# A whole hybrid decoder trunk, its instructions ordered by a different model machine

## Chip, cores and metric

The kernel runs on one core of a Trainium2 chip. The metric is the device time of one execution in microseconds, the median of the runs.

## The reference

Two layers work on a sequence of 512 rows of 1024 channels, in float32. Each layer is a feed-forward half step, a mixing step and another feed-forward half step. Every step begins with an RMS norm that is scaled and shifted by values from a conditioning vector c (`mod = silu(c) @ w_ada + b_ada`), and ends with a gated residual.

```python
hn = rms_norm(h, g_ffn1[l]) * (1.0 + sc1) + sh1
h = h + 0.5 * (1.0 + gt1) * swiglu(hn, w_ffn1_in[l], w_ffn1_out[l])   # 1024 -> 2 x 2816 -> 1024
hn = rms_norm(h, g_mix[l]) * (1.0 + sc2) + sh2
proj = hn @ w_mix_in[l]
mixed = concatenate([attention, rwkv7, short_conv]) @ w_mix_out[l]
h = h + (1.0 + gt2) * mixed
# and a second swiglu with g_ffn2, w_ffn2_in, w_ffn2_out
```

Mixing splits its projection in three: sliding-window attention with sinks over 8 heads, an RWKV-7 recurrence over 4 heads, and a gated short convolution.

## The kernel before

All activations lie transposed, channels on partitions, in 8 tiles `h` of 128 x 512. A float32 weight is not multiplied as it is: ScalarE casts it to a rounded high part `wH` (L101), VectorE subtracts to get the low part `wL` (L102), and TensorE adds up the three products high-high, high-low and low-high (`mm3` from L87, `mm6` from L94). So each weight goes through a load into `wraw` (L267, two buffers), `first`, `third` or `sum` (L391), a cast, a subtraction, and then TensorE; `wH` and `wL` have four buffers each.

The stages follow each other as they are traced: `begin` (the first norm and the first four products, with a number of products of ones to keep TensorE going, `ps_warm`, L1197), then for each layer `ffn`, `mix`, `ffn`. In `ffn`, some row pairs of the inner width are made plainly by `projector`, and the rest by `pair_in`, which saves products by adding weights and activations beforehand; some of these weight sums are made by a DMA that accumulates, issued by GpSimd (L395). The conditioning values are dot products on VectorE (L163), 128 of them over weights that GpSimd's queue loads (`wada`, L177), laid between the other work. In `mix`, `products` yields the big weight products step by step, and three generators, `rwkv(0)`, `rwkv(1)` and `attention`, yield between small products and vector work. A loop with a running credit traces them in turn. The recurrence's part of interest: `ps_o` (L964 to L969), `RT` on VectorE (L971), the copy of `y` on ScalarE (L972), six steps `ps_s` and `St` (L977, L978), `ps_ys` (L983), then a group norm.

What runs when on an engine isn't the traced order. A list scheduler walks through a model machine's time: whenever an engine is free in the model, the ready instruction that was traced first is put next, and buffers of a pool are given out in the same walk. The order it finds is then fixed for each engine's queue, with semaphores for what depends on another engine. Only in some places is the order laid down by hand: regions `tc.manual_schedule` (for instance in `close`, for VectorE and ScalarE, and around some groups of small products) and `tc.issue_after`. The model machine thus decides the rest of the order.

## Time and profile before

| | us |
|---|---|
| median of 3 runs (lowest, highest) | 1912.97 (1912.38, 1913.72) |
| the profiled execution | 1913.21 |
| its span, first to last instruction | 1911.2 |
| TensorE busy | 1878.8 |
| VectorE busy | 1399.8 |
| ScalarE busy | 837.0 |
| GpSimd busy | 130.7 |

Busy time is the union of an engine's instructions. TensorE's matmuls overlap in its pipeline, so a row's mean duration is longer than the distance between two of them. In a row of waits stand the waiting engine, tile and line, what ended the wait, the total in us, the count and the longest. In a row of the order in time stand the start in us, the duration, what ran, the count, and in brackets the idle time of the engine before it with what ended it.

### The profile page before, as it was taken

What the parts mean: (1) busy time and instruction counts of PE and PEld (TensorE: products, weight loads), DVE (VectorE), ACT (ScalarE), POOL (GpSimd) and SP (SyncE); (2) the same over time, 40 slices, a digit from 0 to 9 for tenths busy, and PEclk for the clock granted to TensorE, in tenths of its full rate; (3) what the DMA queues carried; (4) which work ended last, traced back from release to release, by engine and by line L of the source; (5) the groups of instructions that cost most, each with busy time, mean ns of one, the idle gap of its engine ahead of it and who ended that gap; (6) DMA issues with size and microseconds to landing.
All of it is one profiled execution on the core that took longest, in us unless ns stands there. A gap on an engine that the chain in (4) does not pass through costs nothing. (4 is left out here: it accounts for less than half of the span.)

```text
span 1911.2 us, 37042 instructions
## 1 busy us (share of the span) xinstructions
PE 1878.8 (98%) x15504; PEld 1741.7 (91%) x15504; DVE 1399.8 (73%) x2181; ACT 837.0 (44%) x1264; POOL 130.7 (7%) x212
## 2 busy tenths in 40 slices
PE   8999999999999999999999999999999999999999
PEld 7998899897888999899899989989878899988998
DVE  7687687758976877677877776876599667864862
ACT  4443255346322554155345514544562235532551
POOL 0101100100000001110100020010000000110000
PEclk8999999999999999999999999999999999999999
DMA  7767877521312476887727678781321315774741
GB/s 300 245 168 221 271 198 229 168 70 45 79 43 81 123 198 176 278 218 199 264 62 193 171 260 242 191 278 42 93 61 49 88 34 163 209 217 130 198 140 59
DMA packets 104326, 308.46 MB, mean 161 GB/s; under 512 B 23392, under 2 KB 24416, under 8 KB 103136
## 3 DMA queue, kind: packets, MB, share of 16 engines
q1 hardware_dynamic: 75936, 203.33, 32.9%
q0 software_dynamic: 28224, 102.77, 21.7%
q8 instruction: 121, 1.98, 0.4%
q14 instruction: 45, 0.37, 0.1%
HBM read 302.66 MB, written 3.41 MB: 160 GB/s over the span
## 5 line engine op out<-in xcount | busy, mean ns | idle before, releaser
L101 ACT CAST wH<-wraw 128x1024 fp32r<-128x1024 f32 (+2 forms) x292 | 268.4, 922 | 512.6 <-PE ps_mm L91 176.8
L102 DVE TENSOR_TENSOR wL<-wraw,wH 128x1024 fp32r<-128x1024 f32 (+2 forms) x292 | 308.1, 1058 | 96.9 <-ACT wH L101 95.8
L90 PE MATMUL ps_mm<-actH,wH 128*128 128x512 f32 (+1 forms) x784 | 288.5, 368 | 0.0
L91 PE MATMUL ps_mm<-actL,wH 128*128 128x512 f32 (+1 forms) x784 | 288.0, 367 | 0.0
L92 PE MATMUL ps_mm<-actH,wL 128*128 128x512 f32 (+1 forms) x784 | 288.0, 367 | 0.0
L441 PE MATMUL ps_d<-comH,wH 128*128 128x256 f32 x816 | 226.8, 278 | 1.6 <-ACT wH L101 0.8
L443 PE MATMUL ps_d<-comH,wL 128*128 128x256 f32 x816 | 225.8, 277 | 2.3 <-DVE wL L102 2.3
L442 PE MATMUL ps_d<-comL,wH 128*128 128x256 f32 x816 | 225.5, 276 | 0.0
L98 PE MATMUL ps_mm<-hnH,wH 128*128 128x256 f32 x1040 | 214.0, 286 | 5.1 <-ACT hnH L101 2.9
L98 PE MATMUL ps_mm<-hnL,wH 128*128 128x256 f32 x1040 | 211.8, 283 | 0.0
L98 PE MATMUL ps_mm<-hnH,wL 128*128 128x256 f32 x1040 | 209.5, 281 | 0.5 <-DVE wL L102 0.5
L163 DVE SCALAR_TENSOR_TENSOR wada<-wada,crep 128x1024 f32<-128x1024 f32 x140 | 168.0, 1220 | 47.8 <-DMA wada<-in_wadaT 47.6
L102 DVE TENSOR_TENSOR wL<-sum,wH 128x1024 fp32r<-128x1024 f32 x102 | 124.8, 1224 | 74.9 <-ACT wH L101 74.7
L98 PEld LDWEIGHTS ps_mm<-hnH,wH 128*128 128x128 f32 x1040 | 159.5, 190 | 16.1 <-issue 8.2
L92 PEld LDWEIGHTS ps_mm<-actH,wL 128*128 128x128 f32 x784 | 147.8, 189 | 24.4
L90 PEld LDWEIGHTS ps_mm<-actH,wH 128*128 128x128 f32 x784 | 147.8, 189 | 24.2
L91 PEld LDWEIGHTS ps_mm<-actL,wH 128*128 128x128 f32 x784 | 147.8, 189 | 24.1
L101 ACT CAST wH<-sum 128x1024 fp32r<-128x1024 f32 x102 | 107.5, 1054 | 140.3 <-PE ps_d L442 60.1
L98 PEld LDWEIGHTS ps_mm<-hnL,wH 128*128 128x128 f32 x1040 | 160.2, 190 | 6.7 <-issue 5.7
L98 PEld LDWEIGHTS ps_mm<-hnH,wL 128*128 128x128 f32 x1040 | 160.1, 190 | 4.1 <-issue 2.9
L441 PEld LDWEIGHTS ps_d<-comH,wH 128*128 128x128 f32 x816 | 153.2, 188 | 3.9 <-ACT wH L101 1.4
L443 PEld LDWEIGHTS ps_d<-comH,wL 128*128 128x128 f32 x816 | 153.2, 188 | 2.9 <-DVE wL L102 2.9
(402 smaller groups left out, 4237.3 us busy)
## 6 DMA issues: line engine op xcount, KB each, us to landing
wada<-in_wadaT POOLq DMA_DIRECT2D x128, 512.0 KB, 4.9
wraw<-in_wmi SPq DMA_DIRECT2D x40, 512.0 KB
wraw<-in_w2p SPq DMA_DIRECT2D x36, 512.0 KB
wraw<-in_w1p SPq DMA_DIRECT2D x32, 512.0 KB
wraw<-in_w1o SPq DMA_DIRECT2D x32, 384.0 KB
wraw<-in_w2o SPq DMA_DIRECT2D x32, 384.0 KB
wraw<-in_w1i SPq DMA_DIRECT2D x20, 512.0 KB
wraw<-in_w1o SPq DMA_DIRECT2D x32, 320.0 KB
```

The lines of the kernel that those rows point to most:

```text
L90: mm(acc, wH, xH, start=start, stop=False)
L91: mm(acc, wH, xL, start=False, stop=False)
L92: mm(acc, wL, xH, start=False, stop=stop)
L98: mm(acc[:, sl], w[a][:, k], x[b][:, sl], start=start and n == 0 and sl is HALVES[0], stop=stop and n == 2, skip_group_check=True)
L101: nc.scalar.copy(hi, src)
L102: nc.vector.tensor_sub(lo, src, hi.bitcast(F32))
L163: stt(w, w, 1.0, crep, ALU.mult, ALU.mult, accum_out=out_)
L441: mm(pt[:, i], wH, x[k][0], start=start and i + k == 0, stop=False, skip_group_check=True)
L442: mm(pt[:, i], wH, x[k][1], start=False, stop=False, skip_group_check=True)
L443: last = mm(pt[:, i], wL, x[k][0], start=False, stop=k == 3, skip_group_check=True)
```

## The change

The kernel's first statement opens a block that holds the rest of the function, and asks that this block be ordered on the scheduler's other model machine. That one follows the queues, the sequencers and the transfers in time, where the default one has simpler times. The traced program is the same, with the same instructions, tiles, pools and hand-fixed regions. A block is scheduled as a unit; since all of the kernel lies in it, there is nothing outside for it to mix with.

```diff
 def trunk_kernel(ctx, tc, ins, out, layers=L, phases=("ffn1", "mix", "ffn2")):
     nc = tc.nc
+    ctx.enter_context(tc.block(schedule_with_timeline_sim=True))
     PSUM = bass.MemoryType.PSUM
     const = ctx.enter_context(tc.tile_pool(name="const", bufs=1))
     small_ = ctx.enter_context(tc.tile_pool(name="small", bufs=2))
```

## The prediction

> **What bounds the kernel now.** I read the page's first parts, then the busy time of stretches, then the waits of TensorE, and last the order in time around its longest stop.

> ```profile
> span 1911.2 us, 37042 instructions
> PE 1878.8 (98%) x15504; PEld 1741.7 (91%) x15504; DVE 1399.8 (73%) x2181; ACT 837.0 (44%) x1264; POOL 130.7 (7%) x212
> PE   8999999999999999999999999999999999999999
> PEclk8999999999999999999999999999999999999999
> ```

> TensorE is idle for 1911.2 - 1878.8 = 32.4 us of the whole program. That is all that a better order could hand back, beside time lost to a low clock. The profiled execution took 1913.21 us, 2.0 us more than its span and 0.24 us above the median of the three runs, 1912.97. The next view splits the idle time by stage; its columns are the stretch, its length, busy time with counts of each engine, granted clock, DMA share and GB/s.

> ```profile
> 0.00:22.40 22.40, 16.60 (x84) 14.03 (x84) 10.92 (x28) 12.35 (x20) 0.21 (x4) 0.98 0.89 343
> 22.40:37.00 14.60, 12.88 (x73) 12.38 (x74) 14.10 (x24) 6.85 (x10) 0.00 (x0) 0.68 1.02 415
> 399.00:622.00 223.00, 216.17 (x2433) 187.86 (x2434) 166.60 (x341) 92.97 (x193) 0.85 (x4) 1.00 0.24 67
> 1335.00:1558.00 223.00, 215.18 (x2415) 186.81 (x2416) 164.45 (x337) 92.30 (x192) 0.85 (x4) 0.99 0.24 67
> 700.00:750.00 50.00, 50.00 (x443) 50.00 (x443) 37.99 (x42) 27.72 (x36) 4.20 (x6) 1.00 0.67 180
> ```

> The two mixing stages (third and fourth row) hold 6.8 + 7.8 = 14.6 us of idle TensorE, the first 37 us hold 5.8 + 1.7 = 7.5 us, and a stretch in a feed-forward stage (last row) holds none. So the feed-forward stages run at what TensorE gives, and the order of instructions can only matter in the mixing stages and at the start, unless the new order takes away the cover that the feed-forward stages have. How thick is that cover? The waits of ScalarE and of TensorE tell it:

> ```profile
> ACT wH L101 <- PE ps_mm L91: 186.1, 70, 3.5
> ACT wH L101 <- PE ps_d L442: 85.8, 80, 3.7
> PE ps_d L443 <- DVE wL L102: 1.5, 2, 0.8
> PE ps_g L443 <- DVE wL L102: 1.1, 1, 1.1
> L101 ACT CAST wH<-wraw 128x1024 fp32r<-128x1024 f32 (+2 forms) x292 | 268.4, 922 | 512.6 <-PE ps_mm L91 176.8
> L102 DVE TENSOR_TENSOR wL<-wraw,wH 128x1024 fp32r<-128x1024 f32 (+2 forms) x292 | 308.1, 1058 | 96.9 <-ACT wH L101 95.8
> ```

> The weight splits wait for TensorE to give a buffer back (150 of them in the first two rows), not the other way round; TensorE waited for a split only a few times (rows three and four, at the heads of stages). wH and wL have four buffers each, so three weights stand ready when a fourth is freed.

> **The change part by part.** Nothing is added or removed on an engine; only the issue order on each engine can differ, with the buffers that follow from it. There are four places where that can cost.

> *Feed-forward stages.* A weight of a pair step is 24 matmuls of 256 columns; in the rows further below two such matmuls take 0.23 us, so a weight lasts 24 x 0.114 = 2.7 us and three ready ones 8.2 us. A split costs 0.92 + 1.06 = 2.0 us, which leaves some 6 us by which the new order may delay a split before TensorE notices. I take 0. Two rows give the ends: the last fortieth of the span, and the count of pair steps.

> ```profile
> 1863.40:1911.20 47.80, 44.02 (x251) 38.75 (x249) 12.39 (x18) 5.12 (x7) 0.00 (x0) 1.00 0.18 59
> L101 ACT CAST wH<-third x34: 1046/1052/1062, 126.6 to 1835.9; 128x1024 fp32r<-128x1024 f32 x34
> ```

> Of the 32.4 us idle, 14.6 lie in the mixing stages, 7.5 at the start and 47.8 - 44.0 = 3.8 at the end; the remaining 6.5 are the heads of the feed-forward stages, and no more can go there (-6.5). If each of the 34 pair steps paid a stop of the size seen at a stage head, 0.8, it would be +27.

> *Mixing stages.* Here chains of small products (two RWKV heads' groups, attention) are laid between weight products. TensorE's stops here, the first four of eleven rows of its waits between 399 and 622 us (layer 0), and the largest of layer 1:

> ```profile
> PE ps_s L977 <- ACT y L972: 1.4, 1, 1.4
> PE ps_bo L611 <- DVE bonus L800: 0.9, 2, 0.5
> PE ps_ks L611 <- ACT ksq L659: 0.8, 1, 0.8
> PE ps_pt L1057 <- DVE Sc L1050: 0.7, 2, 0.4
> PE ps_s L977 <- ACT y L972: 2.2, 1, 2.2
> ```

> Each such stop is a place where the order puts a chain step earlier than the chip can run it. The opposite error is hidden in these rows: a chain step that stands behind weight products although it is ready. It costs nothing at once, since TensorE works on, but it brings the end of the chain later, and once the weight products are used up that shows as idle time. One product step is six matmuls, three rows of the kind below:

> ```profile
> 1522.04 0.39 PE L98 MATMUL ps_mm<-y3H,wH 128*128 128x256 f32 x2
> 1522.27 0.39 PE L98 MATMUL ps_mm<-y3L,wH 128*128 128x256 f32 x2
> 1522.49 0.39 PE L98 MATMUL ps_mm<-y3H,wL 128*128 128x256 f32 x2
> 1522.72 0.39 PE L98 MATMUL ps_mm<-y4H,wH 128*128 128x256 f32 x2
> ```

> so 1522.72 - 1522.04 = 0.68 us. A chain of `rwkv` has 28 steps (its yields). If the other machine places q of them one product step later, the chain ends 0.68 q later. The two chains run side by side, so a layer pays once. Ends: q = 0, and q = 28, which is 19 us a layer or 38 in both. I take a quarter, q = 7, because the present order was early on the chip in the eleven kinds of places of that view, out of 76 chain steps (two times 28 and attention's 20), about one in seven, and a machine that errs to the other side as well will displace more than that: 7 x 0.68 = 4.8 us a layer, 9.5 us in both.

> *The longest stop.* It sits where the RWKV state recurrence starts, in both layers. VectorE, then ScalarE, then TensorE in layer 1:

> ```profile
> 1524.43 1.23 DVE L102 TENSOR_TENSOR wL<-wraw,wH 128x1024 fp32r<-128x1024 f32 x1 [4.26 <-ACT wH L101]
> 1525.58 0.75 DVE L971 TENSOR_TENSOR RT<-ps_o,AR 128x256 f32<-128x256 f32 x2
> 1523.35 1.05 ACT L101 CAST wH<-wraw 128x1024 fp32r<-128x1024 f32 x1 [5.22 <-DMA wraw<-in_wmo]
> 1526.03 0.70 ACT L972 COPY y<-ps_o 128x256 f32<-128x256 f32 x2 [1.62 <-DVE RT L971]
> 1526.45 0.33 PE L977 MATMUL ps_s<-St,GT 64*64 64x64 f32 x4 [2.17 <-ACT y L972]
> 1526.71 0.73 PE L98 MATMUL ps_mm<-y0H,wH 128*128 128x256 f32 x2
> 1527.24 0.63 PE L98 MATMUL ps_mm<-y0L,wH 128*128 128x256 f32 x2
> 1524.30:1526.40 2.10, 0.00 (x0) 0.00 (x0) 1.97 (x4) 0.48 (x3) 0.00 (x0) 1.00 0.00 0
> 1526.80:1530.20 3.40, 3.40 (x17) 3.06 (x18) 1.50 (x4) 0.66 (x1) 0.00 (x0) 0.50 0.55 146
> ```

> ScalarE's cast waits 5.2 us for a weight's DMA, VectorE's subtraction waits for the cast, and RT, which needs neither, is queued behind it; so the copy y and the first ps_s come late and TensorE stops for 2.17 us (1.4 in layer 0). After it the granted clock is 0.50 for 3.4 us, which is another 1.7 us. A machine that lets that DMA land later would put RT ahead of the subtraction: -(2.2 + 1.4 + 1.7) = -5.3 us. The same machine may as well put new waits of this form elsewhere, at the same price each. I count 0 here and keep -5.3 for a rival.

> [...]

> *The start.* The stretch 22.4 to 37 us ran at a mean granted clock of 0.68. A reordering can cost or save one such half-clock window, 3.4 / 2 = 1.7 us; I take +1.0 since warm-up products placed differently leave a longer stop more easily than a shorter one. Ends -2 and +5 (5.8 us are idle in the first 22.4).

> *The block's entry and exit.* The trace of before has none. Its nearest rows are the first wait of TensorE, for an operand made by an engine that has itself just begun, and the fetching of instructions:

> ```profile
> PE ps_warm L1197 <- ACT ones_r L130: 2.4, 1, 2.4
> q8 instruction: 121, 1.98, 0.4%
> ```

> The fetches go on all through the program beside other work. I take 0, with -1 and +3 as bounds (a second beginning of 2.4 us, rounded up).

> Sum: 1913.2 + 0 (feed-forward) + 9.5 (mixing) + 0 (longest stop) + 1.0 (start) + 0 (block) = 1923.7; less the 0.24 that this execution lies above the median, 1923.5, so 1924.

> **The rivals.** The measurement tells 0.2% (3.8 us) from no change: faster is below 1909.1, slower above 1916.8.

> *Faster.* The machine that follows the queues lets weights land late, so RT goes ahead of the subtraction in both layers (-5.3), and about half of the 6.5 us of feed-forward heads (-3) go with it: 1913.0 - 8 = 1905. For it: the stop is exactly of the form that a model without the DMA's wait would make, and it is there in both layers. Against it: it is only 8 of 32.4 us, and as few as 6 displaced chain steps in all (6 x 0.68 = 4.1 us) bring it back over 1909.1; that is the point from which it decides.

> *No change.* Both machines agree on what is ready where it matters, because in the feed-forward stages the buffers set the order and in the mixing stages the hand-fixed regions do: 1913. Against it: the mixing stages have many places free to move, and 15 us of stops show times that a second machine need not repeat.

> *Feed-forward stages disturbed.* SP and POOL issue in order. If a weight load that waits for a buffer is put ahead of one that could go, or an accumulating load on POOL behind a wada load that waits for VectorE, the cover of 6 us is used up. POOL's queue already stands still long:

> ```profile
> POOL wada L177 <- DVE wada L163: 278.6, 87, 22.4
> POOL third L395 <- DMA third<-in_w2p: 209.9, 16, 35.1
> ```

> With waits of up to 22 us there, one exchange passes through the cover. At one stop of 0.8 us in each of 34 pair steps it is +27 on top of 10.5: 1950; with clock windows lost, more.

> **How the numbers follow.** Mixing stages later (1917 to 1938): 0.40, time 1924. Faster by way of RT and the stage heads (1899 to 1909): 0.27. No change: 0.18. Feed-forward disturbed (1938 and up): 0.15. So faster 0.27, same 0.18, slower 0.55. The range: the faster rival's middle part from 1903, and up to 1955 for the disturbed case's nearer half; about 0.1 is left out at either end. The likeliest case's own range is 1917 to 1938.

> **What would show it.** Right: the stretch of 700 to 750 us still full; the mixing stages' stretches longer than before, with idle time in their last quarter, and ps_s (L977) first started later relative to the stage's begin. RT (L971) standing before the wL that precedes it now would be the faster rival. New rows of TensorE waiting for wL or wH in dozens would be the disturbed case. The sum fails if chain steps move ahead of product steps rather than behind, since then stops shrink or grow without a late chain end, or if the mixing stages' TensorE busy time itself changes because small products are grouped differently.

## The result, and the profile after

The changed kernel takes 1930.33 us (median of four runs, 1928.57 to 1932.86) beside 1913.35 for the kernel before: ratio 1.009, interval [1.0073, 1.0108], 17 us slower. The profiled execution is the fastest of the four, 1928.57 us with a span of 1926.5. Line numbers of the kernel are higher by one than before.

The head of the page and two of its rows by fortieths:

```profile
span 1926.5 us, 37060 instructions
PE 1874.1 (97%) x15504; PEld 1746.0 (91%) x15504; DVE 1392.1 (72%) x2181; ACT 844.1 (44%) x1268; POOL 130.8 (7%) x212
PE   8999999999998999999999999999999989999999
PEclk8999999999999999999999999999999989999999
```

TensorE is idle for 1926.5 - 1874.1 = 52.4 us instead of 32.4, and busy for 4.7 us less. The two eights in the inside of its row are the ends of the two mixing stages.

Stage by stage, from the first `ps_ks` of a mixing stage to the first pair product behind it, and on; before, then after (stretch, length, busy time of TensorE, its weight loads, VectorE, ScalarE and GpSimd, granted clock, DMA share, GB/s):

```profile
399.30:674.10 274.80, 268.27 (x2886) 239.96 (x2887) 210.20 (x413) 121.10 (x235) 2.59 (x6) 1.00 0.28 80
674.10:1335.70 661.60, 656.68 (x4794) 617.86 (x4792) 498.98 (x692) 299.07 (x403) 68.63 (x108) 1.00 0.68 199
1335.70:1612.20 276.50, 269.38 (x2886) 241.00 (x2887) 210.17 (x413) 121.18 (x235) 2.58 (x6) 0.99 0.28 79
1612.20:1911.20 299.00, 294.04 (x2102) 274.80 (x2100) 182.71 (x215) 121.52 (x156) 18.02 (x24) 1.00 0.57 157
```

```profile
399.90:681.70 281.80, 266.54 (x2887) 242.32 (x2888) 208.60 (x412) 123.02 (x236) 2.59 (x6) 0.98 0.26 76
681.70:1345.50 663.80, 656.71 (x4794) 617.75 (x4792) 496.73 (x694) 299.75 (x404) 68.70 (x108) 1.00 0.68 199
1345.50:1627.10 281.60, 266.62 (x2886) 242.36 (x2887) 208.88 (x413) 123.65 (x237) 2.60 (x6) 0.98 0.26 76
1627.10:1926.50 299.40, 293.57 (x2102) 274.53 (x2100) 181.37 (x216) 121.43 (x157) 18.03 (x24) 1.00 0.57 159
700.00:750.00 50.00, 50.00 (x443) 50.00 (x442) 40.26 (x44) 29.46 (x38) 5.07 (x7) 1.00 0.73 192
614.50:617.80 3.30, 3.30 (x17) 3.30 (x17) 0.69 (x1) 0.34 (x1) 0.00 (x0) 0.50 0.00 0
631.50:638.20 6.70, 4.81 (x22) 4.81 (x23) 6.19 (x14) 3.60 (x8) 0.00 (x0) 0.50 0.23 78
```

The mixing stages grew by 7.0 and 5.1 us, the feed-forward stretches by 2.2 and 0.4, everything ahead of the first mixing stage by 399.9 - 399.3 = 0.6: together the 15.3 us between the spans. In the mixing stages TensorE's idle time went from 274.8 - 268.3 = 6.5 to 15.3 us and from 7.1 to 15.0, while its busy time fell by 1.7 and 2.8, although (last two rows) 10 us of layer 0's stage now run at a granted clock of 0.50 (13.7 us of layer 1's, by the trace's record of the clock). The stretch of 700 to 750 us is full as before.

TensorE's largest waits in the changed kernel (waiting tile and line, what ended the wait, total, count, longest), and then the order in time on TensorE around the largest one in layer 0. Its first row is the first step of the first group's recurrence, the next three are steps of the second group's (the first, the second and the last):

```profile
PE ps_mm L99 <- DVE y L1002: 9.6, 2, 4.8
PE ps_mm L91 <- ACT hnH L251: 5.2, 3, 2.1
PE ps_av L1076 <- DVE pmp L1062: 4.3, 4, 1.6
PE ps_o L965 <- DVE N L955: 4.1, 2, 2.8
```

```profile
557.21 0.33 PE L978 MATMUL ps_s<-St,GT 64*64 64x64 f32 x4
...
586.95 0.33 PE L978 MATMUL ps_s<-St,GT 64*64 64x64 f32 x4
590.40 0.33 PE L978 MATMUL ps_s<-St,GT 64*64 64x64 f32 x4
...
602.52 0.33 PE L978 MATMUL ps_s<-St,GT 64*64 64x64 f32 x4
...
614.24 0.69 PE L99 MATMUL ps_mm<-yrH,wH 128*128 128x256 f32 x2 [4.78 <-DVE y L1002]
...
633.39 1.01 PE L91 MATMUL ps_mm<-hnH,wH 128*128 128x256 f32 x3 [2.10 <-ACT hnH L251]
```

The same rows of the two recurrences in the kernel before:

```profile
542.69 0.33 PE L977 MATMUL ps_s<-St,GT 64*64 64x64 f32 x4
...
589.11 0.33 PE L977 MATMUL ps_s<-St,GT 64*64 64x64 f32 x4 [1.36 <-ACT y L972]
591.45 0.33 PE L977 MATMUL ps_s<-St,GT 64*64 64x64 f32 x4 [0.44 <-DVE St L978]
...
598.21 0.33 PE L977 MATMUL ps_s<-St,GT 64*64 64x64 f32 x4
```

The second group's recurrence in layer 0 starts 2.2 us earlier, but from its first step to its last it takes 15.6 us instead of 9.1. By count of the trace, 26, 22, 22, 22 and 22 products of weights stand between the six steps, where before there were 12, 12, 9, 11 and 10. In layer 1 it takes 13.4 us instead of 10.1, with 22, 22, 24, 22 and 5 products between the steps. These products keep TensorE busy, so no wait shows there. But they are the products that were to cover the group norm behind the recurrence: now they are used up, and TensorE stops for 4.78 us until `y` is there, in each layer. A second stop is new in `close`, where the products of the norm (`ps_ss`, `ps_rstd`) stand behind the whole last weight sequence; the next stage's first operand `hnH` comes late by 2.10 us, in each layer.

A third place lies on VectorE ahead of the recurrence; its order in time in the changed kernel, where the first row is the subtraction for the second of the two last output weights:

```profile
574.51 1.23 DVE L103 TENSOR_TENSOR wL<-wraw,wH 128x1024 fp32r<-128x1024 f32 x1 [1.04 <-ACT wH L102]
576.51 3.35 DVE L993 RECIPROCAL gnrs<-gnrs 128x512 f32<-128x512 f32 x1 [0.78 <-ACT gnrs L992]
580.90 0.42 DVE L955 TENSOR_TENSOR N<-ps_gn,pc 128x256 f32<-128x256 f32 x1
585.41 0.75 DVE L972 TENSOR_TENSOR RT<-ps_o,AR 128x256 f32<-128x256 f32 x2
```

The first group's recurrence now starts 557.2 - 399.9 = 157.3 us into the stage, where it was 542.7 - 399.3 = 143.4. So its group norm now meets the second group's setup: its reciprocal takes 3.35 us ahead of `N`, for which `ps_o` waits 2.8 us (the wait list's last row). In the kernel before that reciprocal ran at 553.1 us, long before the second group's `N`.

### The profile page after: what moved, and what is told of

Read it like the earlier page. It is cut to its first block, busy times and chain, and to the rows that moved or that the text cites. A ratio compares the mean times of both kernels' runs of the same rounds, so it can differ in the third digit from the quotient of the medians.

```text
span 1926.5 us, 37060 instructions
## 1 busy us (share of the span) xinstructions
PE 1874.1 (97%) x15504; PEld 1746.0 (91%) x15504; DVE 1392.1 (72%) x2181; ACT 844.1 (44%) x1268; POOL 130.8 (7%) x212
## 3 DMA queue, kind: packets, MB, share of 16 engines
q1 hardware_dynamic: 75936, 203.33, 32.4%
q8 instruction: 121, 1.98, 0.4%
## 4 chain that ended last, share of the span: by engine, by line
PE 83%; DVE 9%; DMA 2%; issue 2%; ACT 2%; SPq 1%; POOL 0%; DVEq 0%; ACTq 0%; POOLq 0%
PE ps_mm L99 17%; PE ps_mm L92 9%; PE ps_mm L91 9%; PE ps_mm L93 9%; PE ps_d L444 6%; PE ps_d L442 6%; PE ps_d L443 6%; PE ps_f L442 3%; PE ps_f L444 3%; PE ps_f L443 3%; PE ps_g L444 2%; PE ps_g L443 2%; PE ps_g L442 2%; DVE wL L103 1%; SPq L860 1%
## 5 line engine op out<-in xcount | busy, mean ns | idle before, releaser
L102 ACT CAST wH<-wraw 128x1024 fp32r<-128x1024 f32 (+2 forms) x292 | 267.5, 921 | 505.9 <-PE ps_mm L92 189.3
L91 PE MATMUL ps_mm<-actH,wH 128*128 128x512 f32 (+1 forms) x784 | 287.6, 368 | 0.3 <-ACT wH L102 0.3
L442 PE MATMUL ps_d<-comH,wH 128*128 128x256 f32 x816 | 225.9, 277 | 0.8 <-ACT wH L102 0.8
L443 PE MATMUL ps_d<-comL,wH 128*128 128x256 f32 x816 | 225.6, 276 | 0.0
L99 PEld LDWEIGHTS ps_mm<-hnH,wH 128*128 128x128 f32 x1040 | 159.6, 189 | 13.4 <-issue 6.2
L91 PEld LDWEIGHTS ps_mm<-actH,wH 128*128 128x128 f32 x784 | 147.8, 189 | 24.4 <-ACT wH L102 0.5
L102 ACT CAST wH<-sum 128x1024 fp32r<-128x1024 f32 x102 | 107.2, 1053 | 117.5 <-PE ps_d L443 73.4
L442 PEld LDWEIGHTS ps_d<-comH,wH 128*128 128x128 f32 x816 | 153.2, 188 | 1.7 <-ACT wH L102 1.4
```

Of the source, the lines that this page charges most:

```text
L91: mm(acc, wH, xH, start=start, stop=False)
L99: mm(acc[:, sl], w[a][:, k], x[b][:, sl], start=start and n == 0 and sl is HALVES[0], stop=stop and n == 2, skip_group_check=True)
L102: nc.scalar.copy(hi, src)
L442: mm(pt[:, i], wH, x[k][0], start=start and i + k == 0, stop=False, skip_group_check=True)
L443: mm(pt[:, i], wH, x[k][1], start=False, stop=False, skip_group_check=True)
```

## The experiments

Theory 1: the place of the chain steps among the weight products, in few places, makes the loss. Rivals: the block as such, VectorE's order, the norm in `close`. All ratios are to the kernel before, run beside each of them (1913.43, 1913.23 or 1913.00 us); gains in us are differences of medians from 1930.33.

| kernel | median us | ratio | interval |
|---|---|---|---|
| the block on the default machine | 1913.19 | 0.9997 | [0.9987, 1.0007] |
| changed, both chains held | 1982.91 | 1.0363 | [1.0349, 1.0377] |
| before, both chains held | 1961.05 | 1.0249 | [1.0235, 1.0263] |
| before, RT first | 1909.79 | 0.9984 | [0.9975, 0.9993] |
| changed, second recurrence held | 1919.95 | 1.0036 | [1.0024, 1.0049] |
| changed, N ahead of the reciprocal | 1924.39 | 1.0066 | [1.0053, 1.008] |
| changed, both of these | 1923.22 | 1.0049 | [1.0037, 1.0062] |
| before, second recurrence late | 1924.68 | 1.0061 | [1.0049, 1.0074] |
| changed, TensorE by hand in `close` | 1923.62 | 1.0051 | [1.0038, 1.0063] |
| changed, held and `close` | 1916.91 | 1.0021 | [1.0012, 1.003] |
| before, RT first and `close` | 1909.74 | 0.9983 | [0.9974, 0.9992] |

**The block alone.** The block without the other machine:

```diff
-    ctx.enter_context(tc.block(schedule_with_timeline_sim=True))
+    ctx.enter_context(tc.block())
```

> The whole kernel in one block, ordered on the default machine; the instruction order of every engine is that of the kernel before, but for the place of the last branch. Theory 1 (the 17 us come from the new order): no entry or exit cost shows, 1913 within 2 us. Rival (the block itself costs, by a branch or by buffers that come free later): 1916 to 1930, with a longer stop of TensorE at the start or end of the program.

0.9997, with the same order on each engine as before. Entry and exit of a block cost nothing that shows (the interval reaches from 2.5 us less to 1.3 us more); the loss is the other machine's order.

**Chain steps held, in both kernels.** Each product step is traced so that it may not be issued ahead of the last `ps_s` group traced before it:

```diff
-                    mm(pt[rows[e]], GT[rows[e], c], St[rows[e], c], start=True, stop=True)
+                    got["hold"] = mm(pt[rows[e]], GT[rows[e], c], St[rows[e], c], start=True, stop=True)
...
-            step = next(prod, "end")
+            with tc.issue_after(got["hold"].ins) if "hold" in got else nullcontext():
+                step = next(prod, "end")
```

> The changed kernel; in each step of the RWKV state recurrence, weight products traced after a ps_s group are queued behind it (order of issue on TensorE alone). Between ps_s groups then stand 6 to 12 product matmuls instead of 22 to 26. Theory 1 (run-ahead of weight products stretches the recurrence, and the products are missing at its end): ps_s groups 1.0 to 1.8 us apart instead of 3.1, the stop before ps_mm<-yr falls from 4.8 us to under 1.5 in both layers, and with the half-clock windows behind it the time falls by 12 to 18 us, to 1912 to 1918. Rival (the recurrence is late for what stands ahead of it, the group norm's reciprocal on VectorE and the late ps_o; the products between its steps cost nothing): the stop before ps_mm<-yr stays above 3 us and the time at 1926 to 1932.

> The same edit on the kernel before, whose order already has 4 to 12 product matmuls between ps_s groups. Theory 1: little to win, 1910 to 1916. Rival (any order closer to the traced one is better, whatever the machine): 1900 to 1908.

Both missed: 1982.91 and 1961.05. The waits of the changed kernel, held:

```profile
PE ps_c L825 <- DVE B L829: 10.4, 2, 5.2
PE ps_pt L1058 <- DVE Sc L1051: 9.8, 5, 4.5
PE ps_o L965 <- DVE St L958: 9.2, 4, 4.4
PE ps_x L917 <- DVE den L1049: 7.5, 1, 7.5
```

The edit touched more than the place in dispute: the first group's recurrence held back the products that fill the stops of the second group's setup and of attention. Where it was meant to act, it did: the wait for `y` ahead of the last weights is 0.4 us. So running products ahead of chain steps isn't bad as such; it pays in one place and costs in another.

**The hold in the second recurrence alone.** The same edit, with `got["hold"]` set only `if q`:

> The changed kernel; only in the second RWKV group's recurrence, which ends last, products traced after a ps_s group are queued behind it. TensorE's order then has 12, 12, 6, 12, 12 product matmuls between its ps_s groups, for 26, 22, 22, 22, 22. Theory 1 (in that recurrence the run-ahead of products is what brings the chain's end late): ps_s groups 1.0 to 1.8 us apart for 3.1, the stop of 4.8 us before ps_mm<-yr under 1.5, time 1914 to 1921. Rival (the stop is owed to what is ahead of the recurrence; the products held back are missed there): the stop at ps_o grows by what the stop before yr loses, 1926 to 1934.

1919.95, in the range of theory 1: 10.4 us of the 17 are back. The first and last of the six steps in layer 0, then the first, third and fourth row of TensorE's waits and the one for `y`:

```profile
587.33 0.33 PE L978 MATMUL ps_s<-St,GT 64*64 64x64 f32 x4
...
595.85 0.33 PE L978 MATMUL ps_s<-St,GT 64*64 64x64 f32 x4
```

```profile
PE ps_mm L91 <- ACT hnH L251: 5.2, 3, 2.1
...
PE ps_o L965 <- DVE St L958: 3.3, 1, 3.3
PE ps_o L965 <- DVE N L955: 3.0, 1, 3.0
...
PE ps_mm L99 <- DVE y L1004: 0.4, 1, 0.4
```

Six steps in 8.5 us, and 0.4 us is left of the 9.6 us of waits for `y`.

**The opposite, on the default machine.** The kernel before, with twice the credit after each step of the second recurrence, so that more products are traced between:

```diff
-                yield 0.6
+                yield 1.2 if q else 0.6
```

> The kernel before, on the default machine, with the credit of a recurrence step of the second group raised from 0.6 to 1.2, so that 24, 18, 18, 24, 24 product matmuls stand between its ps_s groups for 12, 12, 9, 11, 10; all else is as in the kernel before. Theory 1 (this is enough to make the loss): ps_s groups 2.3 to 3.0 us apart, a stop before ps_mm<-yr of 2 to 5 us in each layer with half clock behind it: 1921 to 1930. Rival (the loss needs the rest of the other order): 1912 to 1916.

1924.68, in the range of theory 1: between the steps stand 24, 18, 18, 24 and 24 products, and a stop for `y` comes with them, on the old machine:

```profile
PE ps_mm L98 <- DVE y L1001: 6.8, 2, 3.4
PE ps_s L977 <- ACT y L972: 3.4, 2, 2.2
```

Taken out of the changed kernel the cause gives back 10.4 us, put into the old one it costs 11.5 (1924.68 - 1913.23). That is the main cause, shown from both sides.

**VectorE's order.** N of the second group is put ahead of the first group's reciprocal, alone and with the hold:

```diff
...
+        tc.add_manual_dep(got["gnr0"].ins, got["n1"].ins.name, NOSYNC, reason="N first")
```

> The changed kernel; the first group's long reciprocal of the group norm is queued on VectorE behind N of the second group. Theory 1: the stops of 2.8 and 1.3 us before ps_o go, but the end of the chain gains only as much, so the stop of 4.8 before ps_mm<-yr falls to 2 to 3.5 us: 1922 to 1928. Rival (the chain's end is set by the products between ps_s groups alone): 1928 to 1932.

> Both edits of the two kernels above. Theory 1: no stop over 1.5 us is left in the mixing stages from ps_o to the last product, and what is left of the 17 us is at the heads of stages and in the clock: 1911 to 1918. Rival: as for each alone, no better than 1925.

Alone 6 us come back (1924.39). The stop for `y` was expected to shrink to 2 to 3.5 us and stayed at 4.8; all of the chain only came earlier. With the hold it missed: 1923.22, where 1911 to 1918 was expected. Its runs spread from 1918.67 to 1925.17 and its interval overlaps that of the hold alone, so it isn't shown to be worse than the hold alone, but the two gains don't add. Two new waits stand in its list:

```profile
PE ps_mm L100 <- ACT yrH L103: 4.5, 1, 4.5
...
PE ps_s L979 <- ACT y L974: 3.1, 1, 3.1
```

In layer 0 the reciprocal's 3.35 us now stand between `N` and `RT`, and `ps_s` waits instead of `ps_o`. Moved by one place it can hold up the next one, though with the reciprocal in that place and no hold `ps_s` waits only 0.2 us. What makes the wait for `yrH` stays open. Putting the reciprocal behind the whole recurrence wasn't tried.

**The norm in `close`.** TensorE's order in `close` is fixed as traced, in the changed kernel, in the one with the hold, and in the kernel before:

```diff
-    HAND = {mybir.EngineType.DVE, mybir.EngineType.Activation}
+    HAND = {mybir.EngineType.DVE, mybir.EngineType.Activation, mybir.EngineType.PE}
```

> The changed kernel; in close, TensorE's instructions too are issued as they are traced, so that the norm's ps_ss and ps_rstd stand ahead of the last sequence of weight products and not behind all of it. Theory 1 (the other part of the 17 us is the norm at the heads of stages, uncovered because the products that hid it are used up before): the waits of ps_mm for hnH of VectorE-ScalarE's norm (2.1, 2.1 and 1.0 us) go, with the half clock of 6.8 us after two of them: 1921 to 1926, a gain of 5 to 9. Rival (the norm's chain is late for other reasons): the waits stay, 1928 to 1932.

> The products held behind ps_s in the second group's recurrence (as in after_hold1) and the traced order of TensorE in close. Theory 1 (two places make the loss and they add): 1911 to 1916, within 3 us of the kernel before. Rival (they hide each other): 1917 to 1922.

> The kernel before with RT first (as in before_rt) and the traced order of TensorE in close, where its own order differs from the traced one by a few products. Theory 1: no further gain in close, 1908 to 1911. Rival (the norm's heads hold something there too): 1903 to 1907.

Alone 6.7 us come back (1923.62); the wait for `hnH` is replaced by a smaller one, and the mixing stages spend 13.7 us at half clock instead of 23.9:

```profile
PE ps_mm L99 <- DVE y L1002: 9.6, 2, 4.8
...
PE ps_ss L230 <- DVE ss L207: 3.1, 2, 1.8
```

The edit also moves steps elsewhere (in layer 0 now 25, 22, 27, 11 and 0 products stand between the second recurrence's steps), so the 6.7 us aren't the norm's alone.

With the hold, 1916.91: 13.4 of the 17 us, 0.9 above the range of theory 1, next to the rival's (1917), and less than 10.4 + 6.7 = 17.1. The longest wait left is the one behind the reciprocal, whose place costs more there than in the changed kernel (4.1 us in all):

```profile
PE ps_o L965 <- DVE N L955: 8.1, 2, 5.0
```

Why it lies worse there is open, and that it makes up all that is left isn't shown: the half clock at the start also lasts 17.1 us there, and 13.7 in the changed kernel. In the kernel before, the same edit (beside the next one) changes nothing.

**RT first.** In the kernel before, the last weights' split is written out, and the first of the two subtractions is queued behind `RT` (in the trace both then stand behind it):

```diff
+        for m in got["lows"][:1]:
+            for q, r in got["rts"]:
+                tc.add_manual_dep(m.ins, r.ins.name, NOSYNC, reason="RT first")
```

> The kernel before; the subtraction for the low part of the first of the two last output weights is queued on VectorE behind RT of the second RWKV group (order of issue alone). The prediction's price for the stop at ps_s: 1.4 and 2.2 us and 1.7 us of half clock go, so 1908 (-5.3). Rival (the stop is only moved, to the weight product that needs this low part): 1911 to 1915.

1909.79, 3.6 us faster than before and between the price (1908) and the rival (1911). This is the fastest order found; with `close` added (1909.74) it is no faster. The stops of 1.4 and 2.2 us are gone; of the recurrence's waits one row is left:

```profile
PE ps_s L983 <- DVE St L984: 1.0, 1, 1.0
```

## Why the prediction was right or wrong

**Mixing stages: right in kind, and the size is in part luck.** Forecast for them +9.5 us, measured 7.0 + 5.1 = 12.1; in all, forecast +10.5, measured +17.0. The form was as described: chain steps behind products that could wait, no cost at once, idle time in the last quarter when the products are used up. The sizes were not. The sum took seven chain steps in a layer, each one product step (six matmuls) later, from a count of rows of waits that says nothing of how far another machine moves a step. In the second recurrence of layer 0 all five distances between steps grew, by ten to fourteen matmuls each; in layer 1 four grew, by ten to fifteen. That makes the recurrence 6.5 and 3.3 us longer. Since it also starts earlier in the stage, its last step comes 3.7 and 2.1 us later, which is less than the 4.8 us that the sum lets a layer pay. But a layer pays more than the delay of the chain's end, because the terms below come on top. The sign named beforehand, a later first `ps_s`, came for the first group (13.9 and 14.3 us later in the stage); for the second, whose end counts, it came the other way (2.8 and 1.2 us earlier).

**What the sum for mixing left out.** Three terms. The norm in `close` (6.7 us when mended alone) and the reciprocal on VectorE (6 us alone) were not named; with the 10.4 us of the second recurrence they make 23 and not 17, so they overlap. And the granted clock: 10 us of layer 0's stage run at 0.50, with 3.3 + 4.8 = 8.1 us of work in them, so some 4 us are lost (an estimate: half of that work's time; in layer 0 rows of two products start 615.15 - 614.72 = 0.43 us apart at that clock and 618.92 - 618.69 = 0.23 at full clock). Against these stands a gain, where the prediction said its sum would fail: TensorE's busy time changed. It fell by 4.7 us in spite of the lower clock. By count of the trace, TensorE changes between weight products and small products 102 and 100 times in the two mixing stages, where it was 140 in each before; with the hold in the second recurrence it is 104 and 106 times, and it is busy for 1872.0 us. In the old kernel with the late recurrence it is 136 times in each, and 1882.3 us, more than before at hardly fewer changes, so the count alone doesn't set the busy time. That longer runs of one kind save time is a reading of these numbers and not shown. So the total came near the forecast partly because unnamed terms of both signs met.

**The longest stop: gone, but not in the rival's way.** In the changed kernel no row of `ps_s` is left among TensorE's waits. But `RT` doesn't stand ahead of the last weights' subtractions, as the faster rival said. Both are ahead of it still, and far ahead: in layer 0 at 568.7 and 574.5 us, with `RT` at 585.4 (the last two are the first and last row of VectorE's order above), where before the second stood directly ahead of `RT`. Their loads are issued 13 us earlier in the stage, so `RT` no longer stands behind a subtraction that waits for its DMA. The prediction had a later DMA remove this stop; here the DMAs came earlier. The price of the stop by itself is 3.6 us (RT first), not 5.3. It was outweighed by what it was set against, displaced chain steps, of which five and four in one recurrence of each layer were enough.

**Start.** Forecast +1.0, measured +0.6 up to the first mixing stage: nothing to tell. The first 40 us, after and before, show that the order did change there:

```profile
0.00:40.00 40.00, 35.06 (x203) 32.66 (x204) 30.45 (x64) 22.01 (x30) 0.21 (x4) 0.83 0.91 358
```

```profile
0.00:40.00 40.00, 32.47 (x185) 29.40 (x185) 26.97 (x56) 19.20 (x28) 0.21 (x4) 0.87 0.90 358
```

203 matmuls where there had been 185 (second row, before), at a lower clock.

**Feed-forward stages.** Forecast 0, measured 2.2 + 0.4, at the stages' heads; a stop per pair step, the slower rival, did not come, and 700 to 750 us is full. The cover of three ready weights held. The rival started from SP and POOL issuing in order, and two places in the trace of before agree with it: on POOL a `sum` waits 8.12 us until 207.39 us, and three loads of `wada` go directly behind it, at 207.94, though the dot products on the first two of their buffers had ended at 204.2 and 205.4; on SP a load into `wraw` waits until the subtraction on its buffer ends at 649.15 us, and the loads `sum` and `first` go directly behind it, at 649.55 and 650.03.

**Block.** Forecast 0, and the block alone shows none.

**Instructions.** The claim that nothing is added was not quite so: ScalarE's count went from 1264 to 1268. The four are loads of its function tables, 22 in place of 18, at 1.28 us each: 5.1 us more on an engine that is busy for 44% of the span.

What stays open: why the other machine puts 22 products between two steps, and starts the first recurrence 14 us later (its own times aren't in any trace); and why the two mended places give 13.4 and not 17.1 us. A block around one stage alone wasn't tried; the attribution to stages rests on the stretches and the edits.

## What to carry to other kernels

When a list scheduler lays a serial chain among independent work, a full engine says nothing: look at the distance between the chain's steps, and at what is left to cover the stretch behind its end. Work that runs ahead early is cover that is missing late, so fix only the chain whose end is exposed; fixing both chains cost 53 us where fixing one gave 10. Pin single places by hand (a short operation ahead of a long split in the same queue, for instance) rather than trade one model machine for another.

## What the runs showed of the hardware

```profile
611.10:614.50 3.40, 0.26 (x1) 0.26 (x2) 2.91 (x4) 0.28 (x1) 0.00 (x0) 0.98 0.00 0
614.50:617.90 3.40, 3.40 (x18) 3.40 (x18) 0.69 (x1) 0.34 (x1) 0.00 (x0) 0.51 0.00 0
628.10:631.50 3.40, 2.64 (x23) 2.47 (x22) 0.49 (x2) 1.20 (x2) 0.00 (x0) 0.99 0.02 5
631.50:634.90 3.40, 1.51 (x7) 1.51 (x8) 3.22 (x7) 1.47 (x4) 0.00 (x0) 0.50 0.35 111
578.80:582.20 3.40, 0.61 (x9) 0.44 (x11) 3.37 (x7) 0.00 (x0) 0.00 (x0) 1.00 0.00 0
582.20:585.60 3.40, 3.40 (x112) 3.33 (x113) 3.40 (x7) 0.62 (x1) 0.00 (x0) 1.00 0.02 5
```

The stretch that is idle but for 0.26 us of products is followed by one at 0.51. So is the stretch from 628.1 us, with 2.64 us of busy time, part of it the norm's products of a single column (`ps_ss`): the next one is at 0.50. But behind the stop of 2.8 us for `N`, from 579.3 to 582.1 us, the clock stays at 1.00 (last row), where in layer 1 of the kernel before it is 0.50 behind a stop of 2.17 us. So here neither the length of a stop nor the busy time of the stretch ahead tells alone whether the clock falls, and what share or kind of work is enough to keep it up isn't shown.
